# A mixer and expert layer on one core: where the second expert table is split, and where the last score tiles run

## The chip, the cores and the metric

The kernel runs on one core of one Trainium2 chip. The number that counts is the time of one execution in microseconds, taken on the device. The core has five engines, each with a queue of its own that is worked off in order: TensorE (PE, matrix products into PSUM), VectorE (DVE), ScalarE (ACT), GpSimd (POOL) and SyncE (SP, which here only issues transfers). Transfers between memory (HBM) and SBUF run on 16 DMA engines, whichever queue issues them.

## The reference

`x` is 1024 tokens of 1024 channels, with 256 context tokens before it. The layer has two parts, each with a norm and a modulation in front and a residual around it.

```python
x = x + mod[2] * mixer_output(t_lat, context_states(t_ctx), rows, *mix_w)     # 8 HGRN heads, 4 GLA heads, both directions
x = x + mod[5] * peer(modulate(rmsnorm(x, norm_ffn_g[l]), mod[3], mod[4]), *peer_w)
return rmsnorm(x, final_g)

def peer(h, wq, k1, k2, u, v):      # 16384 experts, one row of u and one row of v each
    # 8 retrieval heads: top 16 of 128 keys twice, top 16 of the sums -> 128 experts e and gates g per token
    act = gelu(sum_d x[p, d] * u[e, d])
    out[p] = sum over the 128 experts of g * act * v[e]
```

## The kernel before

Matrices are taken in three products of half-precision parts: a tensor is split into a high and a low f16 half (`split`, L91: ACT writes the high half, DVE the low one), and `mm3` (L96) adds high x high, high x low and low x high in PSUM.

Stage 1, the heads (about 40 to 1480 us). For 8 HGRN heads and 4 GLA heads the columns of `w_in` come in slabs of 1024 x 128 (`slab`, L176: a load into `w32`, a split into `w16`, three buffers each), and `proj` (L333) multiplies them with the tokens. Each projection calls `meanwhile`, which adds PRE times its length to an account, and for each whole unit in it lets the generator `presplit` (L311) do one step: 16 slabs of the branch weights, 8 rows of `w_out` and 16 slabs of `peer_wq` are loaded, split, and stored as halves in DRAM (`br_d`, `wo_d`, `wq_d`) for later stages. The loads are issued by SP (`ld`), the stores by ACT (`st_`).

Stage 2 (1480 to 1880): branch products, output projection, second norm.

Stage 3, the gates (1880 to 2858). The tokens are 8 blocks of 128. Blocks 0, 1, 4 (`GB`) fetch the rows of their chosen experts by indirect loads on POOL (`gathering`): 128 rows of u and 128 of v per block, 512 KB each for the 128 tokens, six row buffers, and one DVE instruction per row (L919 for u, L924 for v). Blocks 2, 3, 5, 6, 7 (`DB`) are computed densely over all 16384 experts: their gates are spread into a table G in DRAM (`gate_block`, L1051: DVE makes one-hot tiles `oh`, PE multiplies them into `pgm`, which has one buffer, ACT writes `gs`, ACT's queue stores `G_d`). Beside this run "early tiles": the u table has 128 tiles of 128 experts; `u_turn` transposes one (`put`), `u_act` multiplies it with the tokens (`ph`) and takes gelu. For 80 of the 128 tiles (`early`) this is done in this stage and the result stored in `act_d`. The generator `prep` yields a number of units for each piece of gate work, and for each U_US of units one early tile and G_E gathered rows are emitted; early tiles that are left come behind it.

Stage 4, the dense experts (2908 to 4228): for 32 groups of 4 tiles, gates of the group are loaded (`gt4`, from G_d), each tile's scores are loaded (`acr`, early tiles) or computed (the 48 "live" tiles), weighed with the gates (`weigh`: DVE, ACT, DVE), the v rows of the tile are loaded and split (`v_tile`, L1144), and the group before is multiplied out (`out_unit`: PE writes `pe`, two buffers, DVE adds it to `acc`, L1162). `feed` spreads the remaining gathered rows over the tiles in proportion to `work`.

The program text is ordered for each engine by a scheduler, which works through the instructions by priority and by when it expects operands and buffers; the queues' orders below are its result. Tiles of one tag share the `bufs` buffers of the tag; the memory of the gate stage's pool is used again by stage 4's.

Of the kernel before, what the change touches and what calls it, by code (L numbers as in the profile page):

```python
# [8 lines left out]
F32 = mybir.dt.float32  # L9
# [9 lines left out]
P = 128  # L19
D = 1024  # L20
# [38 lines left out]
U_US = 6.2  # L59
# [4 lines left out]
PRE = 0.25  # L64
# [3 lines left out]
def tile_layer(ctx: ExitStack, tc: tile.TileContext, x, c, ctxt, c_ctx, ada_w, ada_b, norm_mix_g,  # L68
# [62 lines left out]

    u_r = peer_u[0].rearrange("(e p) d -> e p d", p=NKEY)
# [40 lines left out]
    with ExitStack() as mixers:  # L173
# [137 lines left out]
        def presplit():  # L311

            for j in range(KC):
                for bi, w in ((0, w_br_gla), (1, w_br_hg)):
                    st_(out=br_d[bi * KC + j], in_=slab(w[0], j * P, f"pb{bi}{j}", SW))
                    yield
            for k in range(KC):
                w32 = wi.tile([P, D], F32, name=f"wo32_{k}", tag="w32", bufs=3)
                ld(out=w32, in_=w_out[k * P:(k + 1) * P, :])
                w16 = ws.tile([P, 2, D], F16, name=f"wo16_{k}", tag="w16", bufs=3)  # L320
                split(w32, w16[:, 0], w16[:, 1], SW)
                st_(out=wo_d[k], in_=w16)
                yield
            for j in range(16):
                st_(out=wq_d[j], in_=slab(peer_wq[0], j * P, f"pq{j}", SWQ))
                yield
# [657 lines left out]
    with ExitStack() as st:  # L984
# [136 lines left out]
        while pend is not None:  # L1121
            early_tile()
# [21 lines left out]
    def v_tile(e):  # L1144
        vn = pd.tile([P, D], F32, name=f"vn{e}", tag="vn", bufs=2)
        ld(out=vn, in_=v_r[e])
        v16 = pd.tile([P, 2, D], F16, name=f"v16_{e}", tag="v16", bufs=2 * GR)
        vmark[0] = split(vn, v16[:, 0], v16[:, 1], SV)
        return v16
# [17 lines left out]
    uT = u_turn(live[0], u_load(live[0]))  # L1167
    li = 0
    work = lambda e: 2.1 if e in early else 9.5
# [6 lines left out]
    for g in range(NG + 1):  # L1176
        cur = None
        if g < NG:
# [3 lines left out]
            for j in range(GR):  # L1182
                e = g * GR + j
                if e in early:
                    ac = pu.tile([P, TD], F32, name=f"acr{e}", tag="ac", bufs=3)
                    ld(out=ac, in_=act_d[early.index(e)])
                else:
                    uTn = None
                    if li + 1 < len(live):
                        uTn = u_turn(live[li + 1], u_load(live[li + 1]))  # L1190
                    ac = u_act(e, uT)
                    uT = uTn
                    li += 1
                cur[1][j] = v_tile(e)
                feed(work(e) / 3)
                cur[0][j] = weigh(e, ac, gt4)
                feed(work(e) / 3)
# [55 lines left out]
```

## Time and profile before

| | |
|---|---|
| runs (median, lowest to highest) | 4222.92 us, 4222.7 to 4229.41 us (3 runs) |
| profiled execution | 4229.67 us, span 4228.0 us |
| mean granted PE clock | 0.961 |
| busy: PE, DVE, ACT, POOL | 3884.8, 2938.6, 1430.1, 1683.9 us |
| DMA | 884.64 MB, mean 209 GB/s |

The times are of one execution, on the core's own clock. "Busy" is the time in which an engine has an instruction in work; a matmul's end is modelled, so a busy PE need not be at its peak rate. The granted clock is the share of PE's full 2.4 GHz that it was given; 0.5 is the lower level, 1.2 GHz. The DMA share is the busy share of the 16 DMA engines.

### The profile page before, as it was taken

What the parts mean: (1) busy time and instruction counts of PE and PEld (TensorE: products, weight loads), DVE (VectorE), ACT (ScalarE), POOL (GpSimd) and SP (SyncE); (2) the same over time, 40 slices, a digit from 0 to 9 for tenths busy, and PEclk for the clock granted to TensorE, in tenths of its full rate; (3) what the DMA queues carried; (4) which work ended last, traced back from release to release, by engine and by line L of the source; (5) the groups of instructions that cost most, each with busy time, mean ns of one, the idle gap of its engine ahead of it and who ended that gap; (6) DMA issues with size and microseconds to landing.
All of it is one profiled execution on the core that took longest, in us unless ns stands there. A gap on an engine that the chain in (4) does not pass through costs nothing.

```text
span 4228.0 us, 60334 instructions
## 1 busy us (share of the span) xinstructions
PE 3884.8 (92%) x23802; PEld 2350.2 (56%) x23802; DVE 2938.6 (70%) x5132; ACT 1430.1 (34%) x2194; POOL 1683.9 (40%) x1197
## 2 busy tenths in 40 slices
PE   6999999999999999988999989986899989999997
PEld 2665665656655444445776667763445544444453
DVE  5345446242556414379987799977989999889998
ACT  5344444243343202034543334552222222222222
POOL 2011111010011012127655567635766666666663
PEclk9999999999999999999999999987999999999998
DMA  5222122221223583227887778869989999989996
GB/s 189 78 73 85 56 73 79 74 87 46 87 64 115 162 282 107 99 97 242 295 307 249 254 242 298 305 228 319 329 318 336 321 323 325 316 311 325 328 315 232
DMA packets 435306, 884.64 MB, mean 209 GB/s; under 512 B 28511, under 2 KB 245066, under 8 KB 431438
## 3 DMA queue, kind: packets, MB, share of 16 engines
q0 software_dynamic: 110592, 402.70, 27.3%
q1 hardware_dynamic: 202676, 320.19, 22.6%
q10 hardware_dynamic: 121754, 157.89, 10.6%
q8 instruction: 186, 3.05, 0.3%
q14 instruction: 98, 0.80, 0.1%
HBM read 764.80 MB, written 115.88 MB: 208 GB/s over the span
## 4 chain that ended last, share of the span: by engine, by line
PE 47%; DVE 25%; DMA 11%; issue 8%; ACT 6%; POOL 4%; SPq 0%; ACTq 0%; DVEq 0%; POOLq 0%
PE ph L100 5%; DVE row_False L919 5%; PE pe L100 5%; DVE gacc L924 4%; PE pgm L1065 3%; PE pq L100 3%; PE pj_f0h L100 3%; PE pv_g L100 2%; PE pv_h L100 2%; DMA row_False<-in_peer_u_dram,idx 2%; PE pj_f1h L100 2%; PE pj_m L100 2%; DMA vn<-in_peer_v_dram 2%; DMA acr<-act_d 2%; PE pso L100 2%
## 5 line engine op out<-in xcount | busy, mean ns | idle before, releaser
L100 PE MATMUL pe<-v,w 128*128 128x512 f16 x3840 | 883.8, 392 | 138.7 <-DVE acc L1162 104.7
L100 PE MATMUL ph<-hb,uT 128*128 128x256 f16 (+1 forms) x6144 | 892.2, 303 | 14.6 <-POOL uT L967 10.4
L100 PEld LDWEIGHTS <-uT 128*128 128x128 f16 x6144 | 609.4, 99 | 242.5 <-POOL uT L967 13.1
L100 PEld LDWEIGHTS <-w 128*128 128x128 f16 x3840 | 384.0, 100 | 623.0 <-issue 166.4
L940 POOL DMA_INDIRECT row_False<-in_peer_u_dram,idx x384 | 548.9, 1429 | 274.6 <-DVE row_False L919 169.2
L940 POOL DMA_INDIRECT row_True<-in_peer_v_dram,idx x384 | 503.6, 1311 | 264.1 <-DVE gacc L924 173.1
L924 DVE SCALAR_TENSOR_TENSOR gacc<-row_True,dots,gacc 128x1024 f32<-128x1024 f32 x381 | 539.7, 1416 | 39.4 <-DMA row_True<-in_peer_v_dram,idx 35.8
L919 DVE SCALAR_TENSOR_TENSOR row_False<-row_False,h2n 128x1024 f32<-128x1024 f32 x384 | 496.2, 1326 | 67.1 <-DMA row_False<-in_peer_u_dram,idx 66.7
L967 POOL TENSOR_TENSOR uT<-uf,uT 128x512 f16<-128x512 f32 x256 | 380.8, 1499 | 284.0 <-ACT uf L966 282.6
L93 ACT ACTIVATE v<-vn 128x1024 f16<-128x1024 f32 x128 | 135.1, 1055 | 501.9 <-DMA vn<-in_peer_v_dram 386.7
L979 ACT ACTIVATE ac<-ph 128x256 f32<-128x256 f32 (+1 forms) x256 | 110.1, 438 | 371.8 <-PE ph L100 367.1
L1065 PE MATMUL pgm<-oh 128*128 128x128 f16 x1280 | 176.4, 295 | 53.2 <-ACT gs L1066 38.8
L1066 ACT ACTIVATE gs<-pgm 128x512 f32<-128x512 f32 x160 | 171.0, 1069 | 136.6 <-PE pgm L1065 136.6
L94 DVE SCALAR_TENSOR_TENSOR v<-vn,v 128x1024 f16<-128x1024 f32 x128 | 168.2, 1314 | 50.5 <-ACT v L93 50.3
L1162 DVE TENSOR_TENSOR acc<-pe,acc 128x1024 f32<-128x1024 f32 x155 | 188.6, 1217 | 11.8 <-PE pe L100 11.7
L100 PE MATMUL pj_m<-hb,w_m 128*128 128x512 f16 x768 | 187.4, 401 | 2.3 <-DVE lf_g L86 1.6
L1065 PEld LDWEIGHTS <-oh 128*128 128x128 f16 x1280 | 145.7, 117 | 77.0 <-issue 63.5
L100 PE MATMUL pq<-hb,w_wq 128*128 128x512 f16 x768 | 180.0, 387 | 1.0 <-POOL hb L89 0.8
L964 ACT ACTIVATE uT<-put 128x512 f16<-128x512 f32 x256 | 155.0, 605 | 71.0 <-PE put L961 69.4
L89 DVE TENSOR_TENSOR oh<-iota,rTr 128x1024 f16<-128x1024 f16 x160 | 139.1, 879 | 33.9 <-PE pgm L1065 33.8
L100 PEld LDWEIGHTS <-hb 128*128 128x128 f16 x1536 | 150.2, 98 | 17.8 <-issue 0.3
L966 ACT ACTIVATE uf<-put 128x512 f32<-128x512 f32 x256 | 154.4, 603 | 8.9 <-POOL uT L967 8.8
(364 smaller groups left out, 5531.9 us busy)
## 6 DMA issues: line engine op xcount, KB each, us to landing
un<-in_peer_u_dram SPq DMA_DIRECT2D x128, 512.0 KB
vn<-in_peer_v_dram SPq DMA_DIRECT2D x128, 512.0 KB
G_d<-gs ACTq DMA_DIRECT2D x20, 2048.0 KB
gt<-G_d ACTq DMA_DIRECT2D x32, 1280.0 KB
act_d<-ac ACTq DMA_DIRECT2D x80, 320.0 KB
acr<-act_d SPq DMA_DIRECT2D x80, 320.0 KB
mw<-in_ada_w_dram SPq DMA_DIRECT2D x32, 512.0 KB
w_wq<-wq_d SPq DMA_DIRECT2D x32, 512.0 KB
```

The lines of the kernel that those rows point to most:

```text
L89: eng.tensor_tensor(out=out, in0=in0, in1=in1, op=op)
L94: return V.scalar_tensor_tensor(out=lo, in0=src, scalar=float(scale), in1=hi, op0=ALU.mult, op1=ALU.subtract)
L100: PE.matmul(ps, lhsT=a(k), rhs=b(k), start=n == 0, stop=n == last)
L919: V.scalar_tensor_tensor(out=row, in0=row, scalar=1.0, in1=h2n, op0=ALU.mult, op1=ALU.mult, accum_out=dots[:, s:s + 1])
L924: V.scalar_tensor_tensor(out=gacc[n], in0=row, scalar=dots[:, s:s + 1], in1=gacc[n], op0=ALU.mult, op1=ALU.add)
L940: G.indirect_dma_start(out=row, out_offset=None, in_=src[0], in_offset=bass.IndirectOffsetOnAxis(ap=gsel[n][0][:, s:s + 1], axis=0))
L964: S.activation(hi, pv, AF.Copy, scale=SU)
L966: S.activation(uf, pv, AF.Copy, scale=SU)
L967: pace[0] = G.tensor_tensor(out=lo, in0=uf, in1=hi, op=ALU.subtract)
L1065: PE.matmul(pgm[:, t, :], lhsT=oh[:, 0, :, t], rhs=oh[:, j, :, t], start=j == 2, stop=j == 3)
L1066: S.activation(gs[:, :, t0:t0 + TB].rearrange("p i n -> p n i"), pgm, AF.Copy, scale=SA / SG)
L1162: vmark[0] = V.tensor_tensor(out=acc[n], in0=ps, in1=acc[n], op=ALU.add)
```

## The change

The v table is loaded, split and stored as halves (`v_d`) during the heads, three rows of it and then one step of the old list by turns; PRE goes from 0.25 to 0.95 to get 170 steps done. All these stores are issued by SP. In stage 4 `v_tile` is one load of the halves. U_US goes from 6.2 to 7.2, and early tiles that are left when the gates are done are not run in a row behind them, but are put between the tiles of group 0, two behind each of its first three (`rest`, `todo`); their results are stored to `act_d` as before. `work`, by which the gathered rows are spread, gets other numbers.

```diff
-U_US = 6.2
+U_US = 7.2
-PRE = 0.25
+PRE = 0.95
...
+    v_d = dram.tile([NKEY, P, 2, D], F16, name="v_d")
...
         def presplit():
...
+            def rows(src, dst, sc, nm):
+                w32 = wi.tile([P, D], F32, name=f"w32_{nm}", tag="w32", bufs=3)
+                ld(out=w32, in_=src)
+                w16 = ws.tile([P, 2, D], F16, name=f"w16_{nm}", tag="w16", bufs=3)
+                split(w32, w16[:, 0], w16[:, 1], sc)
+                ld(out=dst, in_=w16)
+
+            def slabs():
...
+                        ld(out=br_d[bi * KC + j], in_=slab(w[0], j * P, f"pb{bi}{j}", SW))
+                        yield
...
+            more = slabs()
+            for e in range(NKEY):
+                rows(v_r[e], v_d[e], SV, f"v{e}")
                 yield
-            for j in range(16):
-                st_(out=wq_d[j], in_=slab(peer_wq[0], j * P, f"pq{j}", SWQ))
-                yield
+                if e % 3 == 2:
+                    next(more, None)
+                    yield
+            yield from more
...
-        while pend is not None:
-            early_tile()
...
     def v_tile(e):
-        vn = pd.tile([P, D], F32, name=f"vn{e}", tag="vn", bufs=2)
-        ld(out=vn, in_=v_r[e])
         v16 = pd.tile([P, 2, D], F16, name=f"v16_{e}", tag="v16", bufs=2 * GR)
-        vmark[0] = split(vn, v16[:, 0], v16[:, 1], SV)
+        ld(out=v16, in_=v_d[e])
         return v16
...
+    rest = [pend, *es] if pend is not None else []
+    todo = []
+    for j in range(GR):
+        todo += [j] * (j in live) + rest[2 * j:2 * j + 2]
+    todo += rest[2 * GR:] + [e for e in live if e >= GR]
...
-    work = lambda e: 2.1 if e in early else 9.5
+    work = lambda e: 3.3 if e in early else 10.7
...
                 cur[0][j] = weigh(e, ac, gt4)
+                if g == 0:
+                    for r in rest[2 * j:2 * j + 2] if j < GR - 1 else rest[2 * j:]:
+                        st_(out=act_d[early.index(r)], in_=next_act(r))
                 feed(work(e) / 3)
```

Two places show how the queues move. The first is SP's queue in the heads, at the third HGRN head; `w_gh`, `w_f0h` and `w_f1h` are slabs of `w_in`, `w_pb` one of a branch weight. Before:

```order
L179 DMA w_gh_1335<-in_w_in_dram 128x8x128
L179 DMA w_pb_1366<-in_w_branch_gla_dram 128x8x128
L179 DMA w_f0h_1540<-in_w_in_dram 128x8x128
L179 DMA w_f1h_1624<-in_w_in_dram 128x8x128
L179 DMA w_pb_1655<-in_w_branch_hgrn_dram 128x8x128
```

And now, with `w_v` a row of the v table and `v_d`, `br_d` the stores:

```order
L180 DMA w_gh_1420<-in_w_in_dram 128x8x128
L319 DMA v_d<-w_v_1279 128x2048
L316 DMA w_v_1479<-in_peer_v_dram 128x1024
L319 DMA v_d<-w_v_1311 128x2048
L180 DMA w_f0h_1625<-in_w_in_dram 128x8x128
L180 DMA w_pb_1656<-in_w_branch_gla_dram 128x8x128
L319 DMA v_d<-w_v_1481 128x2048
L316 DMA w_v_1688<-in_peer_v_dram 128x1024
L316 DMA w_v_1720<-in_peer_v_dram 128x1024
L324 DMA br_d<-w_pb_1658 128x2048
L180 DMA w_f1h_1727<-in_w_in_dram 128x8x128
```

Between two slab loads there are now loads and stores of v rows, and `w_f0h` and `w_f1h` each stand right behind a store.

The second is ACT's queue where the gates end: `gs` is the last gate tile, `G_d` its store, `gt` the load of a group's gates, `v_0` a split v row, `w_0` the first weighed scores. Before:

```order
L1066 ACTIVATE gs_3_24807<-pgm_124_24902 128x4x128
L1068 DMA G_d<-gs_3_24807 128x4096
L1180 DMA gt_24949<-G_d 128x20x128
L93 ACTIVATE v_0_24955<-vn_24953 128x1024
L93 ACTIVATE v_1_25041<-vn_25039 128x1024
L1180 DMA gt_25193<-G_d 128x20x128
L1140 CAST w_0_24959<-acr_24951 128x640
```

And now, with `uT` and `uf` the turned u tile, `ac` the scores of tile 120 and `act_d` their store:

```order
L1080 ACTIVATE gs_3_24997<-pgm_124_25263 128x4x128
L978 ACTIVATE uT_25301<-put_1_25311 128x512
L1082 DMA G_d<-gs_3_24997 128x4096
L980 ACTIVATE uf_1_25317<-put_1_25311 128x512
L993 ACTIVATE ac_25320<-ph_120_25321 128x256
L993 ACTIVATE ac_25320<-ph_120_25347 128x384
L978 ACTIVATE uT_25376<-put_0_25377 128x512
L1220 DMA act_d<-ac_25320 128x640
L1206 DMA gt_25289<-G_d 128x20x128
```

The v splits are gone, and the work of score tiles stands between the last gate tile and the first weighing.

## Rows read from the trace of the kernel before

**Rows 1.** Busy us of each engine by stage, with clock, DMA share, GB/s.
```profile
core 0: us, PE busy (x) PEld busy (x) DVE busy (x) ACT busy (x) POOL busy (x), PEclk, DMA share, GB/s
40.00:1480.00 1440.00, 1380.65 (x9161) 855.24 (x9159) 693.17 (x1142) 550.86 (x780) 183.30 (x101) 0.98 0.28 85
1480.00:1880.00 400.00, 372.67 (x1747) 177.01 (x1748) 159.46 (x801) 60.55 (x105) 62.48 (x57) 0.97 0.43 146
1880.00:2800.00 920.00, 855.90 (x6139) 639.27 (x6140) 820.10 (x1788) 416.71 (x692) 581.15 (x437) 0.98 0.78 273
2800.00:2858.00 58.00, 39.62 (x294) 32.25 (x292) 30.61 (x41) 29.44 (x35) 5.87 (x5) 0.76 0.35 139
2858.00:2908.00 50.00, 16.19 (x77) 8.19 (x78) 28.99 (x40) 12.42 (x18) 22.26 (x15) 0.64 0.89 306
2908.00:4170.00 1262.00, 1161.88 (x6162) 615.61 (x6161) 1147.62 (x1252) 329.27 (x512) 820.31 (x570) 0.96 0.92 321
4170.00:4228.00 58.00, 36.64 (x156) 15.61 (x153) 49.07 (x50) 12.49 (x25) 7.81 (x6) 0.83 0.57 215
2860.00:3020.00 160.00, 119.83 (x593) 59.33 (x594) 137.24 (x190) 38.72 (x55) 104.81 (x69) 0.87 0.95 332
2900.00:3000.00 100.00, 87.45 (x438) 43.35 (x439) 93.67 (x127) 25.30 (x37) 73.90 (x49) 0.93 0.97 348
2680.00:2700.00 20.00, 20.00 (x150) 14.83 (x149) 17.22 (x17) 7.61 (x15) 17.50 (x13) 1.00 0.96 374
```

**Rows 2.** Waits from 2850 to the end: who for whom, us, times, longest.
```profile
PE pe L100 <- DVE acc L1162: 104.7, 27, 9.1
```

**Rows 3.** Waits of SP's queue in the same stretch.
```profile
SPq L1146 <- DVE v L94: 860.9, 123, 22.3
```

**Rows 4.** Instruction groups, 2860 to 4200: busy us, mean ns, idle before, releaser.
```profile
L924 DVE SCALAR_TENSOR_TENSOR gacc<-row_True,dots,gacc 128x1024 f32<-128x1024 f32 x254 | 348.8, 1373 | 4.4 <-DMA row_True<-in_peer_v_dram,idx 1.7
L919 DVE SCALAR_TENSOR_TENSOR row_False<-row_False,h2n 128x1024 f32<-128x1024 f32 x253 | 319.5, 1300 | 22.5 <-DMA row_False<-in_peer_u_dram,idx 22.2
L100 PE MATMUL ph<-hb,uT 128*128 128x256 f16 (+1 forms) x2208 | 309.3, 300 | 0.9 <-ACT ac L979 0.9
L94 DVE SCALAR_TENSOR_TENSOR v<-vn,v 128x1024 f16<-128x1024 f32 x128 | 168.2, 1314 | 50.5 <-ACT v L93 50.3
L93 ACT ACTIVATE v<-vn 128x1024 f16<-128x1024 f32 x128 | 135.1, 1055 | 501.9 <-DMA vn<-in_peer_v_dram 386.7 <-PE pe L100 115.1
L961 PE MATMUL put<-ident,un 128*128 128x128 f32 x344 | 45.1, 273 | 1.2 <-ACT uf L966 1.2
```

**Rows 5.** PE's timeline at the seam: start, us, instruction, idle before and releaser.
```profile
2856.47 1.10 PE L1065 MATMUL pgm<-oh 128*128 128x128 f16 x8 [1.11 <-ACT gs L1066]
2877.97 1.46 PE L100 MATMUL pe<-v,w 128*128 128x512 f16 x3 [20.40 <-ACT w L1140]
...
2907.76 4.50 PE L100 MATMUL pe<-v,w 128*128 128x512 f16 x11 [1.44 <-DVE w L1141]
```

**Rows 6.** DVE's instruction groups for gathered rows in the gate stage, 1880 to 2858.
```profile
L924 DVE SCALAR_TENSOR_TENSOR gacc<-row_True,dots,gacc 128x1024 f32<-128x1024 f32 x127 | 190.8, 1503 | 35.0 <-DMA row_True<-in_peer_v_dram,idx 34.1
L919 DVE SCALAR_TENSOR_TENSOR row_False<-row_False,h2n 128x1024 f32<-128x1024 f32 x131 | 176.6, 1376 | 44.6 <-DMA row_False<-in_peer_u_dram,idx 44.5
```

**Rows 7.** Waits of ACT for a store's landing in the heads, 70 to 1450.
```profile
ACT w_m L93 <- DMA wq_d<-w_pq: 23.7, 5, 8.2
...
ACT w_gr L93 <- DMA wq_d<-w_pq: 2.0, 1, 2.0
```

**Rows 8.** ACT's timeline at one store, then one slab load in the chain of waits.
```profile
541.65 0.33 ACTq L322 DMA_DIRECT2D wo_d<-wo  x1
545.92 1.06 ACT L93 ACTIVATE w_qh<-w_qh 128x1024 f16<-128x1024 f32 x1 [3.22 <-DMA wo_d<-wo]
...
531.60 3.83 DMA w_vh<-in_w_in_dram
```

**Rows 9.** A group of projection matmuls in the page's list of costliest groups.
```profile
L100 PE MATMUL pj_m<-hb,w_m 128*128 128x512 f16 x768 | 187.4, 401 | 2.3 <-DVE lf_g L86 1.6
```

More of the change, by code (lines that the diff above doesn't have):

```diff
@@ L311, in presplit @@
         def presplit():
-            for j in range(KC):
-                for bi, w in ((0, w_br_gla), (1, w_br_hg)):
-                    st_(out=br_d[bi * KC + j], in_=slab(w[0], j * P, f"pb{bi}{j}", SW))
-                    yield
[L317 to L322, printed above, removed]
+            def rows(src, dst, sc, nm):
[5 more added lines that the diff above has]
+            def slabs():
+                for j in range(KC):
+                    for bi, w in ((0, w_br_gla), (1, w_br_hg)):
+                        ld(out=br_d[bi * KC + j], in_=slab(w[0], j * P, f"pb{bi}{j}", SW))
+                        yield
+                for k in range(KC):
+                    rows(w_out[k * P:(k + 1) * P, :], wo_d[k], SW, f"wo{k}")
+                    yield
+                for j in range(16):
+                    ld(out=wq_d[j], in_=slab(peer_wq[0], j * P, f"pq{j}", SWQ))
+                    yield
+            more = slabs()
+            for e in range(NKEY):
+                rows(v_r[e], v_d[e], SV, f"v{e}")
                 yield
-            for j in range(16):
-                st_(out=wq_d[j], in_=slab(peer_wq[0], j * P, f"pq{j}", SWQ))
-                yield
+                if e % 3 == 2:
+                    next(more, None)
+                    yield
+            yield from more
         ahead = presplit()
@@ L1166, in tile_layer, with next_act @@
     live = [e for e in range(NKEY) if e not in early]
-    uT = u_turn(live[0], u_load(live[0]))
-    li = 0
-    work = lambda e: 2.1 if e in early else 9.5
+    rest = [pend, *es] if pend is not None else []
[3 more added lines that the diff above has]
+    todo += rest[2 * GR:] + [e for e in live if e >= GR]
+    if not rest:
+        uT = u_turn(todo[0], u_load(todo[0]))
+    ahead_ = iter(todo[1:])
+    def next_act(e):
+        nonlocal uT
+        en = next(ahead_, None)
+        uTn = u_turn(en, u_load(en)) if en is not None else None
+        ac = u_act(e, uT)
+        uT = uTn
+        return ac
+    work = lambda e: 3.3 if e in early else 10.7
     left = [sum(map(work, range(NKEY))), 256 * len(GB) - done[0]]
@@ L1187, in tile_layer @@
                 else:
[L1188 to L1193, printed above, removed]
+                    ac = next_act(e)
                 cur[1][j] = v_tile(e)
```

## The prediction

> **What bounds the kernel now.** First the table by stage [rows 1]: the reader is to see that TensorE (PE) is busy 1380.65 of 1440 us in the heads while VectorE (DVE) has 693.17 and ScalarE (ACT) 550.86 us, and the DMA engines 28%. In the gate stage (1880 to 2858) and in the last stage (2908 to 4170) three resources stand close together: in the last stage PE 1161.88, DVE 1147.62 of 1262 us and the DMA engines at 92%. Between the two lie 108 us (2800 to 2908) with PE at 39.62 + 16.19 us and a granted clock of 0.76 and 0.64, a mix of the 1.2 and 2.4 GHz levels. Then the waits of the last stage: PE stood 104.7 us for DVE's adding of `pe` into `acc` [rows 2], and the SP queue stood 860.9 us for DVE's half of the v split before it could load the next v row [rows 3]. So there DVE leads, PE follows, and DMA is not far behind. Last the timeline of PE at the seam [rows 5]: the last `pgm` starts at 2856.47, the next PE instruction at 2877.97 after 20.40 us idle, and a steady run begins at 2907.76.
>
> **The change, part by part.** The sum is made on the profiled execution: 4229.67 us, span 4228.0. It lies 6.75 us above the median of the runs shown (4222.92), and I carry the difference over to that median.
>
> *1. Gate stage.* Early tiles are emitted one per 7.2 units instead of 6.2. The generator yields 543.6 units: 2 x 16 + 16 for three routes, five blocks of 4 x 8 x 1.65 = 52.8, four more routes of 16, 8 x (4 x 3.3 + 4 x 1.5) + 14 for the choosing. Before, the 80 tiles are gone at unit 496, and 47.6 units of bare gate blocks are left: this is the stretch from 2800 to 2858. Now 75 tiles spread to the end and five remain. In the order lists 82.0 tiles stood before the last `pgm`, 75.1 do now; gathered rows used there fall from 259 to 242. One tile costs PE 309.3/46 + 45.1/43 = 7.8 us [rows 4]; one row costs DVE (190.8 + 176.6)/258 = 1.42 us [rows 6]. PE: 895.5 (855.90 + 39.62) - 6.9 x 7.8 = 842 us. DVE: 850.7 - 17 x 1.42 = 827 us. Until 2800 the stage ran with PE at 93.0% and DVE at 89.1% of the time. If the even spread keeps these shares to the end, 842 us of PE want 905 us and 827 us of DVE want 928, against 978 now: 50 to 73 us less. If it only runs at 87% of DVE, 28 less. I take 50, the DVE end: the stage ends at 2808.
>
> *2. The seam.* What was missing there is work that needs no gates. Now 6.9 tiles stand between the last `pgm` and the first `pe`, 54 us of PE, which covers the store of G, the load of `gt4` and the first weighing (about 20 us together in [rows 5]); their u loads are in the SP queue ahead of the first v loads, for the first four of them. So PE's first `pe` comes at 2808 + 54 = 2862, where before it was steady at 2908. If the ACT queue, which holds the first weighing's cast between two tiles, stops the tiles for that wait, up to those 20 us are lost again.
>
> *3. The last stage.* Out go 128 ACT splits (135.1 us), 128 DVE splits (168.2 us) and the 50.5 us that DVE stood before them [rows 4]. In come 17 more rows on DVE (17 x 1.32 = 22 us, 1.32 from (348.8 + 319.5)/507) [rows 4], one more tile on PE and about 5 us of `pe` that were done before 2908: PE 1161.88 + 13 = 1175 us, DVE 1147.62 - 168 + 22 = 1002 us. The v bytes do not shrink: a half-split row is 512 KB again. DMA: 321 GB/s x 1262 us = 405 MB, plus 17 rows of 0.524 MB, plus five u loads of 0.524 and five stores of 0.328 (128 x 1024 and 128 x 640 numbers of 4 bytes), less 1 moved in the seam: 417 MB. So DVE drops to 80%, and the DMA engines become the fullest resource. Three prices for the stretch: at today's 321 GB/s 1299 us; at 332, held for 160 us right after the seam, 1256; at 348, held for 100 us, 1198 [rows 1]. PE's floor is 1175. I take 332, since a queue that no longer waits for DVE asks for the DMA engines all the time, as in those 160 us; the bounds are 1198 and 1299. What is late next is the SP queue itself: v loads of a group wait for the `pe` that frees eight buffers, and the loads of u and act rows stand behind them. The end: 2862 + 1256 + 58 (the tail of [rows 1], whose work stays) = 4176, that is 52 below 4228.
> The row for this rate is 348 GB/s at best over 100 us, and 374 over one stretch of 20 us [rows 1]. The Trainium skill (DMA: Bandwidth & Descriptors, Specifications) states about 358 GB/s as what HBM gives to one core; it speaks against hoping for much from relieving DVE, since 321 is 90% of that. By it the stretch could not fall below 417/358 = 1165 us, by the row below 1198; the 20 us row lies above the page's figure, and neither changes my term.
>
> *4. The heads.* 128 v rows are loaded, split and stored here: ACT +135.1, DVE +168.2 us, 134 MB of transfers; 40 slab stores leave ACT's queue for SP's. PE does nothing new. ACT goes from 550.86 to 686, DVE from 693.17 to 861, of 1440 us; DMA from 28% to about 55% (134 MB at 348 GB/s is 386 us). What hides it is PE's 1380.65 us. The cover ends where an ACT or SP instruction waits in order. Two such waits grow. First, all splits write one of three `w16` buffers, and a stored one is free only when its store has landed: issued at 541.65, ACT went on at 545.92 [rows 8]. Over 40 stores ACT stood 87.1 us for this (12 rows, the first and the last in [rows 7]), 2.2 us each; 168 stores make 366. Queued behind each such wait on ACT are the evacuations of `pj`, which has two buffers, so one projection on PE, 24 x 187.4/768 = 5.9 us [rows 9], covers a wait of 4.3. Second, SP: 29 of 81 slab loads of `w_in` now stand right behind a store that waits for DVE's split, and a slab lands 3.83 us after issue [rows 8]. Between the split of a slab and its first evacuation lie two or more other evacuations in 71 of 80 cases (73 before), so most of these delays are covered; the median lead shrinks from 6 to 5. Price: PE's 59 us of idleness grow by nothing at the best (or shrink by 5, as ACT issues 40 stores less), by 38 if they grow with what ACT has to do and wait for, (686 + 366)/(551 + 87) = 1.65; far end 29 x 3.83 = 111 us. I take 15, nearer to the cover than to the exposure.
>
> Sum: -52 + 15 = -37 us: 4193 for an execution like the profiled one, 4186 against the median.
>
> **The rivals.**
> *A. The pace of the last stage stays.* The DMA engines and the SP queue, not DVE, set it: 92% is what they do here over 1262 us. For it: DMA leads after the change, and the v loads now come in bursts of four ahead of the act and u loads. Against: 95% over 160 us. Then 2862 + 1299 + 58 = 4219, and with the heads' 15 it is 4234: +6, or 4229 at the median, no change to speak of; with free heads 4214.
> *B. Slower: the SP queue starves the slabs.* The place is the heads, where PE has only 4% to give. A store that waits for a late split holds the slab load behind it, whose landing (3.83 us) PE then waits out. From 52/3.83 = 14 late slabs on, of the 29 that stand so, the gain is gone; with all 29 it is +111 - 52 = +59: 4282. For it: DVE itself waits in order for PE in the heads, and its splits with it. Against: the lead of 5 projections.
> *C. More.* The DMA engines reach 348 GB/s and the heads are free: 2862 + 1198 + 58 = 4118, or 4113 at the median.
>
> **How the numbers follow.** The forecast, with anything from 4148 to 4214, has 0.46; C (below 4148) 0.17; A 0.20, half of it within 0.2%, the rest evenly to both sides; B 0.17. A change of 0.2% (8.4 us) is about what a measurement of this kernel tells from none. Faster: 0.46 + 0.17 + 0.05 = 0.68. Same: 0.10. Slower: 0.05 + 0.17 = 0.22. The range from 4135 to 4240 leaves out the lower half of C and the upper two thirds of B, 0.09 and 0.11.
>
> **What would show it.** Right: the last `pgm` near 2810 plus what the heads lost, no stretch without gathers before it, no PE pause of 20 us behind it; in the steady stretch DVE near 80%, DMA at 94 to 96%, PE's wait for `acc` below 50 us, SP's wait for v gone; in the heads PE idle for about 75 us instead of 59. Wrong: heads that end over 50 us later, with ACT or PE waiting for `w16` and slabs (B); DMA still at 92% with DVE idle (A); or a gate stage that is not shorter by 28.

## The result and the profile after

The changed kernel takes 4257.68 us (median of 4 runs, 4253.89 to 4271.23), the kernel before beside it 4223.81: the ratio is 1.0083, with a 95% interval from 1.0059 to 1.0107. It is slower by 0.8%, outside the spread of the runs, and lies above the range that was given. The profiled execution (4253.89 us, the shortest of the four) has a span of 4250.8 us, 22.8 more than the profiled execution of before. The medians lie 33.9 apart, so the sum by stages below explains 23 of these 34 us.

The table by stage of the changed kernel, cut where the stages begin (window and its length in us; busy time and instructions of PE, PE's weight loads, DVE, ACT, POOL; granted PE clock, DMA share, GB/s):

```profile
core 0: us, PE busy (x) PEld busy (x) DVE busy (x) ACT busy (x) POOL busy (x), PEclk, DMA share, GB/s
40.00:1546.40 1506.40, 1401.59 (x9162) 860.60 (x9161) 856.18 (x1269) 677.48 (x908) 188.67 (x101) 0.96 0.53 172
...
1546.40:1944.10 397.70, 372.65 (x1755) 177.61 (x1755) 160.69 (x807) 60.55 (x105) 62.36 (x57) 0.97 0.42 143
1944.10:2857.30 913.20, 838.86 (x6030) 630.51 (x6029) 817.39 (x1802) 423.92 (x684) 541.10 (x410) 0.98 0.75 265
2857.30:2926.50 69.20, 56.58 (x391) 39.90 (x389) 32.55 (x23) 23.15 (x46) 39.92 (x28) 0.93 0.92 330
2926.50:4193.00 1266.50, 1175.79 (x6235) 624.05 (x6236) 1033.46 (x1160) 217.38 (x398) 794.78 (x590) 0.96 0.90 327
4193.00:4250.80 57.80, 37.81 (x165) 16.44 (x163) 49.10 (x50) 12.50 (x25) 6.62 (x6) 0.86 0.57 209
```

And the kernel before, cut at the same places:

```profile
40.00:1482.20 1442.20, 1380.65 (x9161) 855.24 (x9159) 694.16 (x1143) 550.86 (x780) 183.30 (x101) 0.98 0.28 86
...
1880.80:2857.30 976.50, 894.46 (x6425) 670.72 (x6423) 849.91 (x1824) 445.75 (x726) 587.03 (x442) 0.96 0.75 265
2857.30:2907.80 50.50, 16.25 (x80) 8.11 (x78) 28.79 (x40) 12.62 (x18) 22.26 (x15) 0.64 0.88 302
```

One against the other, with the last stage from [rows 1]: the heads end at 1546.4 instead of 1482.2, 64.2 us later. Of these, 43.3 are more idle time of PE (1442.2 - 1380.65 = 61.6 before, 1506.4 - 1401.59 = 104.8 now), and 20.9 are more busy time for the same matmuls, at a granted clock of 0.96 instead of 0.98. The merge stage is unchanged. The gate stage takes 913.2 instead of 976.5 us, 63.3 less: PE has 55.6 us less to do in it (838.86 against 894.46) and idles 7.7 less. From the last `pgm` to the first steady `pe` it is now 69.2 us instead of 50.5; the steady stretch takes 1266.5 instead of 1262.2, the tail 57.8. So +64.2 - 0.9 - 63.3 + 18.7 + 4.3 - 0.2 = +22.8.

In the heads, the waits of ScalarE that ended with a transfer (total, times, longest, us):

```profile
ACT w_v L93 <- DMA v_d<-w_v: 80.7, 28, 7.0
ACT w_v L93 <- DMA w_v<-in_peer_v_dram: 35.4, 15, 8.7
ACT w_pb L93 <- DMA v_d<-w_v: 22.6, 4, 10.8
ACT w_qh L93 <- DMA v_d<-w_v: 18.6, 4, 6.1
ACT w_pq L93 <- DMA v_d<-w_v: 17.9, 7, 6.4
```

`w_v L93 <- v_d<-w_v` reads: the high half of a v row could not be written until the store of an earlier row in the same buffer had landed. The slabs (`w_pb`, `w_qh`) stand for v rows' stores too, since all share three buffers. Added up over all such rows, ACT stood 249 us for landings of stores and 118 for loads; before it was 100 and 28 (a part of it in [rows 7]). How such a wait reaches PE is seen once in the timeline at 94 us (start, duration, engine, line, instruction, and the idle time ahead of it):

```profile
87.18 1.16 DVE L94 SCALAR_TENSOR_TENSOR w_v<-w_v,w_v 128x1024 f16<-128x1024 f32 x1
88.36 0.34 SPq L319 DMA_DIRECT2D v_d<-w_v  x1
...
92.41 1.06 ACT L93 ACTIVATE w_pb<-w_pb 128x1024 f16<-128x1024 f32 x1 [10.83 <-DMA v_d<-w_v]
93.37 0.58 ACT L585 ACTIVATE at_f0h<-pj_f0h 128x512 f32<-128x512 f32 x1
...
94.00 1.44 PE L100 MATMUL pj_f1h<-hb,w_f1h 128*128 128x512 f16 x3 [4.25 <-ACT at_f0h L585]
```

DVE finishes its half late, SP issues the store at 88.36, it lands about 4 us later, only then may ACT split the branch slab (which nobody needs yet), and behind that stands the evacuation of `pj`, for which PE has waited 4.25 us. Over all the heads, the rows of PE's waits that grew most are these:

```profile
PE pj_f1h L100 <- ACT at_f0h L585: 15.5, 4, 4.3
PE pmd L693 <- DVE macc L685: 9.8, 1, 9.8
PE pmd L693 <- DVE mbb L89: 6.7, 2, 5.9
```

Added up, PE's waits for ACT in the projections (`pj`, `pv`) go from 0.9 to 22.5 us. Its waits for the sums of the modulation (`pmd`), at the end of the heads, go from 0.8 to 16.5 us: DVE adds up rows (`macc`) which SP loads between stores of v rows. These two are 37 of the 43 us.

The seam, PE's timeline: there is no pause of 20 us any more, as there was in [rows 5], but there is one of 8.51.

```profile
2856.51 1.10 PE L1079 MATMUL pgm<-oh 128*128 128x128 f16 x8
2857.43 6.05 PE L100 MATMUL ph<-hb,uT 128*128 128x256 f16 x42
...
2886.77 2.09 PE L975 MATMUL put<-ident,un 128*128 128x128 f32 x8 [8.51 <-ACT uf L980]
...
2921.47 2.32 PE L100 MATMUL pe<-v,w 128*128 128x512 f16 x10
2926.53 3.97 PE L100 MATMUL pe<-v,w 128*128 128x512 f16 x10 [2.74 <-ACT w L1152]
```

The 8.51 us are the loss that the prediction named as possible on ACT's queue: the first weighing's cast stands there between two tiles and waited 13.61 us, and the copies out of `put` stood behind it.

```profile
2885.00 0.72 ACT L1152 CAST w<-acr 128x640 f16<-128x640 f32 x1 [13.61 <-DVE acr L89]
```

The waits of the last stage (2857.3 to 4193), DVE's and PE's:

```profile
DVE acr L89 <- DMA acr<-act_d: 100.2, 36, 6.7
PE pe L100 <- DVE acc L1172: 90.0, 30, 5.7
DVE row_False L933 <- DMA row_False<-in_peer_u_dram,idx: 58.9, 31, 10.2
```

The split is gone and DVE is busy 82% of the steady stretch instead of 91%, yet PE waits for the adding of `pe` nearly as long as before [rows 2]: DVE now stands for stored score tiles (`acr`) and gathered rows.

### The profile page after: what moved, and what is told of

It reads as the page before. It is cut to its first block, busy times and chain, and to the rows that moved or that the text cites. A ratio compares the mean times of both kernels' runs of the same rounds, so it can differ in the third digit from the quotient of the medians.

```text
span 4250.8 us, 60803 instructions
## 1 busy us (share of the span) xinstructions
PE 3904.6 (92%) x23802; PEld 2356.0 (55%) x23802; DVE 2959.1 (70%) x5132; ACT 1433.5 (34%) x2194; POOL 1634.1 (38%) x1197
## 4 chain that ended last, share of the span: by engine, by line
PE 38%; DVE 22%; DMA 18%; issue 10%; ACT 6%; POOL 5%; SPq 0%; ACTq 0%; DVEq 0%; POOLq 0%
PE pe L100 4%; DMA row_False<-in_peer_u_dram,idx 4%; DMA acr<-act_d 4%; DVE row_False L933 4%; PE ph L100 4%; DVE gacc L938 3%; PE pgm L1079 3%; PE pj_f1h L100 2%; DMA gt<-G_d 2%; PE pv_g L100 2%; PE pso L100 2%; DMA v_d<-w_v 2%; PE pq L100 2%; DVE eqr L89 2%; POOL row_False L954 2%
## 5 line engine op out<-in xcount | busy, mean ns | idle before, releaser
L954 POOL DMA_INDIRECT row_False<-in_peer_u_dram,idx x384 | 506.5, 1319 | 275.2 <-DVE row_False L933 174.7
L933 DVE SCALAR_TENSOR_TENSOR row_False<-row_False,h2n 128x1024 f32<-128x1024 f32 x384 | 505.2, 1348 | 100.5 <-DMA row_False<-in_peer_u_dram,idx 99.6
L94 DVE SCALAR_TENSOR_TENSOR w_v<-w_v,w_v 128x1024 f16<-128x1024 f32 x128 | 169.0, 1321 | 191.4 <-ACT w_v L93 191.1
L93 ACT ACTIVATE w_v<-w_v 128x1024 f16<-128x1024 f32 x128 | 134.9, 1055 | 173.1 <-DMA v_d<-w_v 80.7
L89 DVE TENSOR_TENSOR acr<-acr,gt 128x640 f32<-128x640 f32 x80 | 76.6, 974 | 143.1 <-DMA acr<-act_d 100.2
```

The lines of the kernel that those rows point to most:

```text
L89: eng.tensor_tensor(out=out, in0=in0, in1=in1, op=op)
L94: return V.scalar_tensor_tensor(out=lo, in0=src, scalar=float(scale), in1=hi, op0=ALU.mult, op1=ALU.subtract)
L933: V.scalar_tensor_tensor(out=row, in0=row, scalar=1.0, in1=h2n, op0=ALU.mult, op1=ALU.mult, accum_out=dots[:, s:s + 1])
L954: G.indirect_dma_start(out=row, out_offset=None, in_=src[0], in_offset=bass.IndirectOffsetOnAxis(ap=gsel[n][0][:, s:s + 1], axis=0))
```

## The experiments

Times of a stage are those of each run's profiled execution; "after the last `pgm`" is from that instruction to the end of the span (1370.7 us before, 1393.5 after).

**The two halves of the change alone.** First the hand-over without the v split: the changed kernel with `presplit`, `v_tile` and PRE as before.

> The changed kernel with the v split put back where it was before (v loaded and split in the last stage, PRE 0.25, the old list of slabs and stores); the slower spread of early tiles, the hand-over of the rest to group 0 and the new numbers of the gather spread stay. Theory 'the parts add up' (the heads' loss belongs to the v split, the gate stage's gain to the spread): heads end at 1482 as before, gate stage 913 against 976.5, seam about 69, last stage's steady stretch 1262 plus the PE work of the tiles handed over, 1275; end 4196 of a span like 4228, ratio 0.992. Rival 'VectorE pays': without the v split out of the way the 17 more gathered rows raise VectorE's work in the last stage from 1148 to 1170 us and the stretch with it, to 1286: ratio 0.995. Rival 'the gate gain needs the rest': gate stage back near 950 or more, ratio 1.00.

Measured: 4212.45 us, ratio 0.9976 (0.9967 to 0.9986), span 4217.4. The heads end at 1478.5.

```profile
1877.60:2786.80 909.20, 838.82 (x6030) 630.51 (x6030) 817.93 (x1804) 424.46 (x684) 548.59 (x410) 0.98 0.76 266
2786.80:4217.40 1430.60, 1278.97 (x6789) 683.76 (x6787) 1266.08 (x1360) 373.03 (x596) 885.56 (x624) 0.94 0.90 314
```

The gate stage is shorter by 67 us, and 60 of them come back after it: 64 us of PE work more stand there than before (1278.97 against 1214.96), and PE still idles 152 us. The hand-over moves work; it saves about 7 us, and more was expected. The steady stretch took 1305.7 us, more than the first theory's 1275 and the rival's 1286. This is the only version tried that computes all of the reference's products and is faster than the kernel before, by 0.24%.

Then the v split without the hand-over:

```diff
-U_US = 7.2
+U_US = 6.2
-    work = lambda e: 3.3 if e in early else 10.7
+    work = lambda e: 2.1 if e in early else 9.5
```

> The changed kernel with the spread of the early tiles as before (6.2, so none is handed over, and the old numbers of the gather spread); only the v split in the heads stays. If the parts add up and the relief of VectorE brings nothing in the last stage: heads end 64 us late (1546), gate stage 976, from the last pgm to the end 1371 + 58 less or more 10; ratio 1.015. Rival 'the relief does count, but the hand-over ate it' (17 rows and a tile more in the last stage): the steady stretch falls from 1262 to 1215 to 1240, ratio 1.004 to 1.010.

Measured: 4277.03 us, ratio 1.0122 (1.0102 to 1.0143). Heads at 1545.8, after the last `pgm` 1360.8 us: 64 lost, 10 won. The steady stretch took 1253.0 us, so the rival's 1215 to 1240 was not reached. Beside the hand-over the split's absence is worth more in the last stage (1430.6 - 1393.5 = 37 us). Neither covers 64.

**Whose order costs the heads?** The stores back on ACT's queue:

```diff
-                ld(out=dst, in_=w16)
+                st_(out=dst, in_=w16)
...
-                        ld(out=br_d[bi * KC + j], in_=slab(w[0], j * P, f"pb{bi}{j}", SW))
+                        st_(out=br_d[bi * KC + j], in_=slab(w[0], j * P, f"pb{bi}{j}", SW))
```

> The changed kernel with the stores of all split halves issued by ScalarE's queue, as before, instead of SyncE's. Theory 'SyncE's order' (a store that waits for a late split holds the slab load behind it, and PE waits for the slab): the heads end 30 to 60 us earlier than 1546, at 1490 to 1515, and ScalarE's waits for w_in slabs at wv_h and wv_g (26 us) go; ratio 0.994 to 1.001. Rival 'ScalarE's own work and waits' (split buffers free only when their store has landed, evacuations queued behind): the heads end within 10 us of 1546, or later by ScalarE's 168 issues; ratio 1.006 to 1.012.

Measured: 4341.79 us, ratio 1.0270 (1.0255 to 1.0286); heads at 1627.9, ACT's waits for landings 393 us instead of 249. The first theory was wrong: far from holding the slabs back, SP's queue saved 82 us. The rival had the direction and not the size. That pointed to ScalarE's waits, so the next runs took these apart. With the v rows' stores taken from a tile that is constant in the heads, the split buffers are free at once:

```diff
-                ld(out=dst, in_=w16)
+                if nm[0] == "v":
+                    ld(out=dst.rearrange("p a (k t) -> p a k t", k=2), in_=hb[0][:, :, 0:2, :])
+                    return
+                ld(out=dst, in_=w16)
```

> The changed kernel with the v rows still loaded and split in the heads, but the 128 stores into v_d take their bytes from a tile that is constant in the heads, so that a split buffer is free at once and no store waits for a split (v_d holds other values: the v halves are left out of the result). Bytes, issues and engine work stay. Theory 'landing' (ScalarE stands in order until the store of a split buffer has landed, and PE's evacuations stand behind it): the heads end at 1482 to 1510 instead of 1546, ScalarE's waits for v_d landings (137 us or more) gone, PE's waits from 104 back to about 60. Theory 'engine work' (303 us more of ScalarE and VectorE instructions between evacuations): heads still at 1535 to 1550. Theory 'transfers' (twice the DMA traffic makes slabs late): heads at 1535 to 1550 too. The rest of the kernel as in the changed one.

Measured: heads at 1505.2, ratio of the whole 0.9964 (0.9951 to 0.9978).

```profile
40.00:1505.20 1465.20, 1383.21 (x9162) 856.97 (x9161) 848.83 (x1271) 679.39 (x908) 187.56 (x101) 0.98 0.54 176
```

Of the 41 us, 22.8 are idle time of PE and 18.4 its busy time, at a granted clock of 0.98 again. PE's waits in the projections fall to 11.4 us and those for `pmd` to 4.5. The second run leaves out `w16` and `split` of the v rows as well.

> As the run with the stores from a constant tile, and the 128 splits of v are left out as well (v rows are loaded and nobody reads them, the same bytes are stored; the v halves are left out of the result). What is left of the change in the heads is 134 MB of transfers and 256 issues on SyncE. Theory 'landing': the heads end within 10 us of that run. Theory 'engine work': heads at 1485 to 1500, some 50 us earlier than that run. Theory 'transfers': heads at 1530 to 1550 in both.

Measured: heads at 1489.6, ratio 0.9946 (0.9924 to 0.9969).

```profile
40.00:1489.60 1449.60, 1381.33 (x9161) 855.38 (x9160) 691.94 (x1143) 551.95 (x780) 182.16 (x101) 0.98 0.55 178
```

So the 64 us come apart, taken out in this order: 134 MB of transfers and 256 issues cost 7, the splits themselves 16, and what the store does to its buffer and to SP 41. The six profiles in which the heads' program text is that of the changed kernel end them between 1545.3 and 1549.6, so a difference of 4 us is not told from none. To part the buffer's share from SP's, SP was made to wait for every split while the buffer stays free:

```diff
...
+                    one = hp.tile([1, 1], F16, name=f"one_{nm}", tag="one", bufs=16)
+                    V.tensor_copy(out=one, in_=w16[0:1, 1, 0:1])
+                    ld(out=s_d[int(nm[1:])], in_=one)
                     ld(out=dst.rearrange("p a (k t) -> p a k t", k=2), in_=hb[0][:, :, 0:2, :])
...
```

> As the run with the stores into v_d from a constant tile (heads 1505 there, 1546 in the changed kernel), but SyncE still has to wait for every v split: behind each split VectorE copies one element into a small tile, and SyncE stores that one (2 bytes) to a scratch row. So the split buffers are free at once, while SyncE's queue still stands for VectorE's splits (the v halves are left out of the result as there). Theory 'landing' (the 41 us are ScalarE standing until a stored split buffer has landed): heads end at 1500 to 1515. Theory 'SyncE's order' (the 41 us are slab loads held behind SyncE's wait for a split): heads end at 1535 to 1550.

Measured: heads at 1508.3. The row of the table of the heads:

```profile
40.00:1508.30 1468.30, 1386.70 (x9162) 856.26 (x9161) 855.50 (x1399) 679.22 (x908) 183.91 (x101) 0.98 0.53 176
```

With the same splits and the same DMA share as after, PE idles 81.6 us instead of 104.8 and has its clock of 0.98 again. SP's queue stood 426 us for v splits here, 353 in the run before it (which has to wait for free load buffers) and 469 in the changed kernel. So 73 of the 116 us of SP's waiting were put back, and they cost 3 us, no more than the spread. The landings have the rest, some 38 by subtraction; the other 43 us of SP's waiting were not tested apart from them. Does a fourth buffer help? With a load buffer given up for it:

```diff
-            w32 = wi.tile([P, KC, P], F32, name=f"w32_{nm}", tag="w32", bufs=3)
+            w32 = wi.tile([P, KC, P], F32, name=f"w32_{nm}", tag="w32", bufs=2)
...
-            w16 = ws.tile([P, 2, KC, P], F16, name=f"w16_{nm}", tag="w16", bufs=3)
+            w16 = ws.tile([P, 2, KC, P], F16, name=f"w16_{nm}", tag="w16", bufs=4)
...
```

> The changed kernel with four split buffers (w16) instead of three and two load buffers (w32) instead of three; to make room, three one-hot buffers instead of four in the gate stage, so only the heads are read. Theory 'landing': a buffer comes round later, ScalarE's waits for landings fall from 240 us by a third or more and the heads end at 1515 to 1535. Theory 'SyncE's order': loads can run less far ahead of use, heads at 1546 or later.

Measured: heads at 1575.2. ACT's waits for landings fell from 249 to 95 us, as expected, but those for loads rose from 118 to 315:

```profile
ACT w_v L93 <- DMA w_v<-in_peer_v_dram: 133.8, 57, 6.5
```

The expected gain was wrong. The reading behind it can stand if what counts is how long ACT stands in order, whatever for; the table below speaks for that. With three load buffers kept (room from one `y16`, two `msg`, three `oh` buffers and smaller constants):

> The changed kernel with four split buffers (w16) instead of three and still three load buffers; room for it by one y16 buffer instead of two, two msg buffers instead of four in the merge stage, three one-hot buffers instead of four, and smaller constants. Theory 'landing': ScalarE's waits for landings in the heads fall from 249 us to 100 to 150, those for loads stay near 118, and the heads end at 1510 to 1530 (PE's waits 104 to 85). Rival 'the waits only move' (as with two load buffers, where ScalarE's waits for loads grew from 118 to 315 and the heads ended at 1575): loads' waits grow by as much, heads within 10 us of 1546.

Measured: heads at 1524.0, ratio of the whole 1.0050 (1.0033 to 1.0067). The 22 us are in the expected size; 15.0 of them are PE's busy time (1386.59 against 1401.59, clock 0.97). ACT's waits for landings fell less than expected, to 223, of which 37 are those of the single `y16` buffer. These runs together, in us:

| run | ACT's waits for landings | for loads | heads end |
|---|---|---|---|
| before | 100 | 28 | 1482.2 |
| no split, constant store | 105 | 49 | 1489.6 |
| constant store | 79 | 125 | 1505.2 |
| constant store, SP waits | 96 | 112 | 1508.3 |
| 4 split buffers | 223 | 114 | 1524.0 |
| after | 249 | 118 | 1546.4 |
| 4 split, 2 load buffers | 95 | 315 | 1575.2 |
| stores on ACT's queue | 393 | 85 | 1627.9 |

The end follows the sum of the two columns, from 128 to 478, in exactly this order. That is an order and not a price: the runs differ in more than these waits. Last, the v splits on GpSimd, which has little to do in the heads:

```diff
-                split(w32, w16[:, 0], w16[:, 1], sc)
+                if nm[0] == "v":
+                    tsc(G, w16[:, 0], w32, sc, ALU.mult)
+                    tsc(G, w32, w32, sc, ALU.mult)
+                    tt(G, w16[:, 1], w32, w16[:, 0], ALU.subtract)
+                else:
+                    split(w32, w16[:, 0], w16[:, 1], sc)
```

> The changed kernel with the 128 v splits of the heads made by GpSimd (three instructions a row, of the size of its 2 us products here) instead of ScalarE and VectorE; buffers and queues as they are. Theories 'landing' and 'engine work' both expect an earlier end of the heads, 1485 to 1520, since ScalarE neither waits for the v buffers nor works on them; ratio 0.995 to 1.003. Rival 'GpSimd is late itself': its own products for the heads (qe, ke, lf; 200 us) stand behind splits that wait for landings, and PE waits for them: heads at 1546 or later, ratio 1.008 or more.

Measured: 4815.79 us, ratio 1.1406 (1.1382 to 1.1430), heads at 2108.7. The rival was right, and its size far beyond: GpSimd needs 2.88 us for each of the two scalings and 2.23 for the subtraction, and its waits for loads and landings come on top (up to 1900 us, both scalings in one row):

```profile
L84 POOL TENSOR_SCALAR w_v<-w_v 128x1024 f16<-128x1024 f32 x236 | 679.9, 2881 | 513.6 <-DMA w_v<-in_peer_v_dram 132.9 <-DMA v_d<-w_v 85.6 <-issue 55.9
L89 POOL TENSOR_TENSOR w_v<-w_v,w_v 128x1024 f16<-128x1024 f32 x117 | 261.4, 2234 | 9.0
```

**The split in the merge stage.** On top of the hand-over alone, 48 v rows are split between the merge stage's steps, with one or two generator steps per merge step and three per output tile, and the other 80 in the last stage. Their loads and halves share three buffers, and SP issues both loads and stores:

```diff
...
+            more_v(1 + hf)
...
+                more_v(3)
...
```

> The slower spread and the hand-over alone (heads as before), and 48 of the 128 v rows split between the merge stage's steps (1480 to 1880), where ScalarE is busy for 15% and VectorE for 40% of the time; the other 80 are split in the last stage as before. If a row split early is worth there what the changed kernel shows (37 us for 128 rows), the last stage is 14 us shorter than in the run of the hand-over alone (1431 from the last pgm to the end), and if the merge stage's PE covers the rows (398 us stay below 403): ratio 0.993 to 0.995. Rival 'the same trap': the merge stage's loads stand behind stores that wait for splits, it grows by 15 us or more: ratio 0.998 or above.

Measured: 4236.31 us, ratio 1.0028 (1.0016 to 1.0039).

```profile
1491.80:1911.10 419.30, 378.25 (x1755) 180.89 (x1756) 209.97 (x848) 102.83 (x147) 64.39 (x57) 0.94 0.70 245
```

What follows the last `pgm` won 23 us against the run of the hand-over alone (1407.3), more than expected; the merge stage grew by 21, and began 13 later. The trace has the reason for the 13 us:

```profile
1491.83 6.82 PE L100 MATMUL pb_g<-yin0g,w_bg 128*128 128x512 f16 x24 [14.10 <-DMA yin0g<-yg_d]
...
1487.02 0.33 SPq L806 DMA_DIRECT2D v<-in_peer_v_dram  x1
1487.45 5.18 SPq L828 DMA_DIRECT2D yin0g<-yg_d  x8
```

PE was done with the heads at 1478 and stood 14.10 us for the merge stage's first load, which SP issued only at 1487.45, behind loads and stores of v rows (in the kernel before at 1477.30, and PE stood 2.61 us). The rival held, at the stage's start too; within it ACT stood 130.1 us for v loads.

**What holds the last stage?** Three runs on loads, then one on PE's work. The score tiles' loads on ACT's queue:

```diff
-                    ld(out=ac, in_=act_d[early.index(e)])
+                    st_(out=ac, in_=act_d[early.index(e)])
```

> The changed kernel with the loads of the stored score tiles (acr) in the last stage issued by ScalarE's queue instead of SyncE's, where they stand behind v and u loads that wait for buffers. Theory 'order of the queue': VectorE's wait for acr falls from 99 us below 30, PE's wait for the adding of pe from 90 to 50 or less, the steady stretch from 1266 to 1230 or less; ratio below 1.000. Rival 'the transfers' rate is the bound': VectorE's wait for acr falls too, but its wait for gathered rows, gt and v grows by as much, PE's wait stays near 90 and the stretch within 12 us of 1266; ratio 1.005 to 1.011. ScalarE's queue may itself hold the loads behind activations that wait: then acr's wait stays near 99.

Measured: ratio 1.0107 (1.0089 to 1.0125), 1398.1 us after the last `pgm`; DVE's wait for `acr` 105.8. The time is the rival's, but `acr`'s wait did not fall. The trace shows what the expectation named last: ACT's queue held the loads, which stand there right behind evacuations of live tiles (`ac<-ph`), and these follow PE. Five `ac` buffers instead of three (and three `oh` buffers):

> The changed kernel with five buffers for score tiles (ac, acr) instead of three, so that loads of stored tiles can be issued earlier; to make room, three one-hot buffers instead of four in the gate stage, so only what follows the last pgm is read (1393.5 us to the end in the changed kernel). Theory 'order of the queue': VectorE's wait for acr falls from 100 us below 40, the time after the last pgm to 1370 or less. Rival 'rate': the wait for acr falls, those for rows or gt grow, the time stays within 10 us of 1393.

Measured: 1396.9 us after the last `pgm`:

```profile
DVE acr L89 <- DMA acr<-act_d: 105.9, 37, 6.9
PE pe L100 <- DVE acc L1172: 91.4, 31, 7.4
```

So the number of buffers is not it. The order of the queue is not ruled out by these two runs, for in neither could the loads start freely. With five buffers too, each of the 43 u loads of the steady stretch is followed on SP's queue by a load of `acr`, and SP stands for PE's `put` before the u load as long as in the changed kernel (the first row is of the changed kernel, the others of the run with five buffers):

```profile
SPq L966 <- PE put L975: 577.4, 43, 25.9
...
SPq L966 <- PE put L975: 570.9, 43, 21.1
...
3231.49 0.33 SPq L966 DMA_DIRECT2D un<-in_peer_u_dram  x1
3231.91 0.86 SPq L1212 DMA_DIRECT2D acr<-act_d  x2
```

Half of the v bytes:

```diff
-        ld(out=v16, in_=v_d[e])
+        ld(out=v16[:, 0], in_=v_d[e][:, 0])
...
-                lambda k: vts[k][:, 0, hs], lambda k: vts[k][:, 1, hs], nk=GR)
+                lambda k: vts[k][:, 0, hs], lambda k: vts[k][:, 0, hs], nk=GR)
```

> The changed kernel with only the high half of each v row loaded in the last stage, the products with the low half made with the high half instead (the low half of v is left out of the result): 33.5 MB of some 414 less, all PE work kept. Theory 'the transfers' rate is the bound of the last stage': the steady stretch falls by up to 33.5 MB / 327 GB/s = 102 us towards PE's 1176 busy us, to 1180 to 1210, VectorE's waits for acr (99 us) and rows (59 us) shrink by half or more. Rival 'the engines' order' (PE, VectorE and the gathers wait for each other in order whatever the rate): the stretch stays within 20 us of 1266, and PE's wait for the adding of pe near 90.

Measured: ratio of the whole 0.9938 (0.9921 to 0.9955), 1347.0 us after the last `pgm`, 46.5 less, between the two theories; 18.5 of them are PE's busy time (1251.71 against 1270.18, clock 0.97 against 0.95). DVE's wait for `acr` fell to 68.7 us and PE's for `acc` to 60.2, that for gathered rows only to 54.9. Then PE's work, a third of `pe` left out:

```diff
-            mm3(ps[:, hs], lambda k: wts[k][:, 0, ns], lambda k: wts[k][:, 1, ns],
-                lambda k: vts[k][:, 0, hs], lambda k: vts[k][:, 1, hs], nk=GR)
+            for k in range(GR):
+                for a in range(2):
+                    PE.matmul(ps[:, hs], lhsT=wts[k][:, 0, ns], rhs=vts[k][:, a, hs],
+                              start=k + a == 0, stop=k == GR - 1 and a == 1)
```

> The changed kernel with the third of the three products of the last stage (low half of the weights by high half of v) left out: PE loses a third of its pe work there, some 285 of 1232 us after the last pgm; every transfer and all work of VectorE and ScalarE stay. Theory 'PE leads the last stage' (92% busy, the rest waiting for the adding of pe): the time from the last pgm to the end falls from 1393.5 by 100 us or more, until VectorE (1066 us) or the transfers stop it. Theory 'the transfers' rate or the chain of loads leads': it falls by less than 40 us, and PE just waits longer.

Measured: 1278.5 us after the last `pgm`, 115 less, ratio of the whole 0.9795 (0.9774 to 0.9816).

```profile
2925.00:4080.00 1155.00, 949.20 (x5077) 515.36 (x5075) 1020.98 (x1166) 217.88 (x404) 794.74 (x586) 0.93 0.97 359
...
3750.00:3850.00 100.00, 84.84 (x456) 45.88 (x455) 91.38 (x112) 20.00 (x37) 69.56 (x51) 0.95 1.00 377
```

The same transfers, with nothing of DVE's work left out, went through in some 110 us less, at 359 GB/s. PE had 252 us less to do (1018.48 against 1270.18), so something else stops the gain at 115: PE's wait for `acc` rose to 206.9 us, and the DMA engines are at 0.97. So in the changed kernel PE leads the last stage, with the transfers close behind: taking work from either shortens it, taking the v split from DVE and ACT does so by 10 to 37 us.

## Why the prediction was wrong

- **The heads, part 4, are the step that failed: +64 where it had +15.** It saw the wait for landings and its place (ACT, behind it the evacuations of `pj`), and put 366 us as the sum of such waits at the old 2.2 us per store. That was too much: ACT stood 249 us for landings, 240 of them for the 168 stores. It put nothing for ACT's waits for loads, which rose from 28 to 118. What was wrong was the cover: "nearer to the cover than to the exposure" rested on a wait of up to 4.3 us being hidden by one projection. With 128 of the stores taken off the split buffers, the heads end 41 us earlier, so the waits were not hidden. They are not alike: the longest was 10.8, since a store also waits for DVE's half, which stands in order behind DVE's own work. PE's idle time grew by 43 us, and 21 more of the 64 are PE's own busy time at a granted clock of 0.96 instead of 0.98, which goes with the waits (below) and has no term in the sum. The bound that scaled PE's idle time with ACT's load, +38, comes near the 43 by luck: with the measured 240 in the place of 366 it gives 27.
- **Rival B had the place and the direction but not the mechanism.** It named slabs held behind SP's stores, and the sign of being wrong that goes with it (heads over 50 us later, ACT waiting for `w16`) came. The run in which SP waits for every split and the buffers are free puts SP's waiting at 3 us, as far as that run brings it back. Having the stores on SP's queue and not on ACT's was worth 82 us for all 168; the prediction saw 5 at most in ACT's 40 old issues.
- **The gate stage, part 1, was right**: -63 where it had -50, inside the stated 50 to 73. DVE's share, by which it went, held (89.5% for 89.1%), with 817 us of work where it had 827.
- **The seam, part 2**: 69 us where it had 54. The pause did go, as it said, and PE's work there is the 54 us of the sum (56.58, at a clock of 0.93). The other 12.6 us are waits, most of them the one behind the first cast on ACT's queue, which the text named and did not price in.
- **The last stage, part 3**: 1266.5 where it had 1256, so its size was nearly right and its reason was not. The rate of 332 GB/s is no limit: the run with less PE work moved 359 over 1155 us, and 377 in a stretch of 100 us at a DMA share of 1.00, so the 348 that the text drew from a row was too low a bound. The Trainium skill (DMA: Bandwidth & Descriptors, Specifications) has about 358 as the limit that HBM sets to one core. The mean of 359 agrees with it, the stretch at 377 does not, so here it is no ceiling. The DMA share was to be 94 to 96% and was 90, less than the 92 of before. "There DVE leads, PE follows" is the reading that failed: in the run without the hand-over, where only the v split is gone from the last stage, the time after the last `pgm` fell by 10 us; with a third of PE's `pe` gone it fell by 115. Of rival A's two limits, the rate of the DMA engines is out by the same run; the SP queue stays open (below). PE's wait for `acc` was to fall below 50 us and stayed at 90: the wait for the v split became a wait for `acr` and gathered rows.
- **The sum**: +49 in the heads, -13 in the gate stage, +15 at the seam, +10 in the last stage against the terms, 61 in all, and 1 less in the stages that had none: from -37 to +23.

What stays open is why `acr` is late in the last stage. Fewer bytes reduced the wait to 69 us. The order of SP's queue, where its loads stand behind u loads that wait for PE, is a cause that the rows allow and that no run took away: the run with the loads on ACT's queue put them behind other waits, and the run with five buffers left them in their place.

## What to carry to other kernels

Work that is moved "into the shade" of a busy engine has to pass through the in-order queues of the engines that feed it: count each added wait by what stands behind it on that queue, not by the engine's busy share, and look for the buffer that is freed only by a landing. Moving work past a seam shortens one stage and lengthens the next; add up the leading engine's busy time over both before counting a gain. If a feeder is relieved and the leader is 92% busy, price the relief by the leader's idle time that names this feeder, and expect only a part of it.

## What the runs showed of the hardware

- With a third of `pe` left out, the DMA engines carried 359 GB/s at a share of 0.97 over 1155 us, and 352 over all that follows the last `pgm`; the changed kernel moved 327 at a share of 0.90 in its steady stretch.
- GpSimd took 2.88 us for a 128x1024 scaling of f32 (the mean of scalings to f16 and to f32) and 2.23 us for a subtraction, where DVE does its half of the split in 1.32.
- The granted clock went with PE's pauses in the heads, which the prediction did not price: the same 9162 PE instructions took 1401.59 us at 0.96 with 104.8 us of idle time and 1386.70 at 0.98 with 81.6. Two neighbouring stretches of the changed kernel, the first without a pause and the second with 3.3 us of them, stand at the full clock and at a mix of the two levels:

```profile
1020.00:1060.00 40.00, 40.00 (x307) 27.60 (x308) 12.79 (x17) 16.24 (x21) 0.00 (x0) 1.00 0.54 170
1060.00:1100.00 40.00, 36.73 (x174) 19.09 (x173) 15.81 (x17) 22.90 (x28) 9.80 (x4) 0.87 0.24 80
```

Not every stretch with a pause shows it (1260 to 1300 had 36.44 us busy at 1.00), so this is a tendency and no rule.
